# Hybrid encoder layer on one core: the MLP's split features move to the left stage pool of SBUF, its squared features to the right one

## The chip, the cores and the metric

The kernel runs on one core of a Trainium2 chip. The metric is the device time of one execution in microseconds (us). Beside it stands a profile of one execution, with its own time.

## The reference, cut to what matters

One encoder layer on 512 tokens of width 1024, all in float32: adaLN vectors, a mixer (a Hyena branch and a dilated attention branch, one output projection), a residual, and then the part that the change touches, the MLP:

```
h = rmsnorm(x, g_pre_mlp) * (1.0 + sc2) + sh2          # (512, 1024)
f = jnp.square(jax.nn.relu(h @ w_mlp1)) @ w_mlp2       # hidden width 4096
x = x + gt2 * rmsnorm(f, g_post_mlp)
```

## The kernel before, in words

**Precision.** Every matmul operand is split into a high and a low part of type fp32r (`whi`/`wlo` for weights, `h2h`/`h2l` for the normalised input of the MLP, the two halves of a tile `ha` for the hidden features). A product is three matmuls (`mm3`, line 610): high by high, high by low, low by high. ScalarE (ACT) makes the high part by a copy, VectorE (DVE) or GpSimd (POOL) the low part by a subtraction (`lo_of`, line 607).

**The MLP in blocks.** `hidden` (line 1392) computes one of 8 blocks of 512 hidden features: 8 x 4 x 3 matmuls of 128x128 by 128x512 into four PSUM banks `pm` (block 0 in two halves of 256 columns), then for each bank ACT applies the relu into a tile `hid` and DVE squares it in place. A `hid` tile holds two banks' worth, `[128, 2, 512]` float32, 4 KB of each partition.

The blocks are used in pairs. `products` (line 1492) takes one pair as a 2 x 2 block matrix and computes it with seven products in the manner of Strassen and Winograd, instead of eight. Each product reads two `ha` tiles (4 KB each), which `split_a` (line 1420) makes from `hid` or from a difference `dif` of `hid` tiles; it is 4 x 2 x 3 = 24 matmuls into two banks `pf`, with a slice of `ha` as the stationary operand and 512 columns of a weight tile as the moving one. Three pairs go that way; between the products lie the quarter blocks of the next pair (lines 1561 to 1567). The fourth pair (lines 1571 to 1598) is done directly: eight tiles `ha` in the list `parts` (one for every 128 hidden features), 2 x 8 x 4 x 3 = 192 matmuls, and after it the norm and the store of the output.

**Where tiles lie.** Two tile pools are shared out by stages. The left region, above the fixed pools, holds in turn `basis`, `wx` and, in the MLP, `hp`; the right region, at the upper end of SBUF, holds in turn `xp`, `hT`, `att` and, in the MLP, `mp` (lines 578 to 581). A pool opens when nothing of the pool before it is in use any more. In the program before, the byte addresses in each partition are: tag `cv` (among others `h2h`, `h2l`, and the filters' `fh`, the Hyena's `th`) 26,464 to 71,520; tags `vx` and `w` (weights `whi`, `wlo`) 92,000 to 135,008; tag `qk` (the tiles `nb`) 135,008 to 151,392; tag `H` (`mh`, `ml` in the output projection) 151,392 to 169,824; left region (`fb` in `basis`, output weights in `wx`, then `hp`) 171,872 to 196,512; right region (`hh`, `hl` in `hT`, `ma` in `att`, then `mp`) 196,576 to 229,344.

Before, `hp` holds 6 slots of `hid` and `mp` 8 slots of `ha`:

```
two = plan.tile("hp", "hid", 6, [P, 2, 512], F32, "hid")     # line 1408, in hidden
a = plan.tile("mp", "ha", 8, [P, 2, 2, 256], F32R, "ha")     # line 1423, in split_a
a = plan.tile("mp", "ha", 8, [P, 2, 512], F32R, "ha")        # line 1573, the last pair
```

**What sets the order.** Every operation is recorded and then put in order by a list scheduler (`Plan.order`, line 291): at each step it takes, over the engines, the operation that can start first by its own estimates of durations, with priorities by the longest path behind it and by a bonus that falls from one product or quarter block to the next (`begin`, line 1458). A new tile needs a free slot of its tag, and only the first tiles in recorded order, as many as there are free slots, may take one (`slot_time`, line 331). The engines then work in that order, each one in sequence.

Of the kernel before, what the change touches and what calls it, by code (L numbers as in the profile page):

```python
# [11 lines left out]
F32 = mybir.dt.float32  # L12
F32R = mybir.dt.float32r
# [12 lines left out]
P = 128  # L26
# [533 lines left out]
def tile_hymba_layer(ctx, tc, t, out):  # L560
    nc = tc.nc
    plan = Plan(nc)
# [23 lines left out]
    def S(tag, s="u", dt=F32):  # L586
        return plan.tile(HOME.get(tag, "up"), tag, NB[tag], [P, 512], dt, s)

    def R(tag, s="r"):
        return S(tag, s, F32R)  # L590
# [16 lines left out]
    def lo_of(eng, lo, full, hi):  # L607
        eng.tensor_tensor(out=lo, in0=full, in1=f(hi), op=ALU.subtract)

    def mm3(ps, lh, ll, rh, rl, start, stop):  # L610
        pe.matmul(ps, lh, rh, start=start, stop=False)
        pe.matmul(ps, lh, rl, start=False, stop=False)
        pe.matmul(ps, ll, rh, start=False, stop=stop)
# [8 lines left out]
    def wload(src):  # L622
        raw = S("raw", "raw")
        pre_loads.append(sp.dma_start(raw, src))
        hi, lo = wpair()
        act.copy(hi, raw)
        lo_of(vp, lo, raw, hi)
        return hi, lo
# [291 lines left out]
    for tt in range(4):  # L920
        for hf in range(2):
            a = S("x", "x")
# [18 lines left out]
    for d in range(8):  # L941
# [3 lines left out]
        a = S("vx", "xnT")  # L945
# [6 lines left out]
    for c in range(4):  # L952
# [4 lines left out]
        for d in range(2 * c, 2 * c + 2):  # L957
            hi = R("h", "hh")
            lo = R("h", "hl")
            a = xnT[d]  # L960
# [208 lines left out]
    for tt in range(4):  # L1169
        b3 = vb[tt].rearrange("p (h d) -> p h d", h=NH)  # L1170
        for g in range(2):
            a = R("cv", "vh")
# [84 lines left out]
    for hp2 in range(4):  # L1257
        (qh, ql), (kh, kl) = qk[hp2]
        a = S("vx", "att")
# [57 lines left out]
    for tt in range(4):  # L1317
        for hf in range(2):
            a = S("qk", "xr")
# [72 lines left out]
    def hidden(cc, banks, res):  # L1392

        for kk in range(0, 8, 2) if cc else (0,):
            if cc == 0:
                ws = [wload(w_1[k * P:(k + 1) * P, 0:512]) for k in range(8)]
            else:
                ws = {k: wload(w_1[k * P:(k + 1) * P, cc * 512:cc * 512 + 512]) for k in (kk, kk + 1)}
            for ts in HALF if cc == 0 else (slice(0, 512),):
                for k in range(8) if cc == 0 else (kk, kk + 1):  # L1400
                    for i in range(4):
                        s = slice(i * P, (i + 1) * P)
                        mm3(banks[i][:, ts], ws[k][0][:, s], ws[k][1][:, s], h2T[k][0][:, ts], h2T[k][1][:, ts], k == 0, k == 7)
            if kk < 6 and cc:
                yield
        for i in range(4):
            if i % 2 == 0:
                two = plan.tile("hp", "hid", 6, [P, 2, 512], F32, "hid")
                res.append(two)
            r = two[:, i % 2]  # L1410
            act.activation(r, banks[i], AF.Relu)
            vp.tensor_tensor(out=r, in0=r, in1=r, op=ALU.mult)
        yield
# [6 lines left out]

    def split_a(src):

        a = plan.tile("mp", "ha", 8, [P, 2, 2, 256], F32R, "ha")
        act.copy(a[:, 0], src)
        lo_of(vp, a[:, 1], src, a[:, 0])
        return a
# [28 lines left out]
    hid = {cc: [] for cc in range(2 * NS)}  # L1455
# [7 lines left out]
    def block(cc):  # L1463
        plan.group += 1
        gen = hidden(cc, PS4(cc == 0, "pm"), hid[cc])
        for _ in range(4 if cc else 1):
            begin()
            next(gen)
            yield
# [22 lines left out]
    def products(sb):  # L1492
# [45 lines left out]
        def first(k):  # L1538

            a = split_a(minus(0, A21, A22, k))  # L1540
            minus(2, A11, X[0], k)
            minus(1, A21, A11, k)
            return a

        same = lambda A: lambda k: split_a(A[k])
        product(3, same(A11), load("b", 0, 1))
        yield
# [6 lines left out]
        product(1, same(X[2]), more("s", 1, 1))  # L1554
        yield
        product(7, lambda k: split_a(minus(0, A12, X[2], k)), more("d", 1, 0))
        yield
        product(6, same(X[1]), more("s", 0, 1))
# [11 lines left out]

    parts = []
    for kk in range(8):
        a = plan.tile("mp", "ha", 8, [P, 2, 512], F32R, "ha")
        src = hid[2 * NS - 2 + kk // 4][kk % 4 // 2][:, kk % 2]
        act.copy(a[:, 0], src)
        lo_of(vp, a[:, 1], src, a[:, 0])
        parts.append(a)
    BLOCK = {(0, 0): 7, (0, 1): 5, (1, 0): 2, (1, 1): 6}
    for hf in range(2):
        plan.group += 1  # L1580
        banks = PS4(1 - hf, "pf")
        for ks, tts in (((0, 1, 2, 3), ((0, 1, 2, 3),)), ((4, 5, 6, 7), ((0,), (1,), (2,), (3,)))):
            begin()
            ws = [wload(w_2[(NS - 1) * 1024 + k * P:(NS - 1) * 1024 + (k + 1) * P, hf * 512:hf * 512 + 512]) for k in ks]
            for us in tts:
# [7 lines left out]
                a = acc[BLOCK[tt // 2, hf], tt % 2]  # L1593
# [48 lines left out]
```

## Time and profile before

| | before |
|---|---|
| time, median of 3 runs | 733.45 us (733.18 to 733.83) |
| the profiled execution's own time | 732.56 us |
| its span, first to last instruction | 730.8 us |
| PE (TensorE matmul) busy | 705.9 us, 97% of the span, 3576 instructions |
| DVE, ACT, POOL busy | 536.4, 357.9, 149.5 us |
| chain that ended last | PE 85%, DVE 6%, DMA 4%, ACT 3% |

Busy time is the union of an engine's instructions. Matmuls overlap in the records (each is shown from its start to the modelled end of its results), so the time that one costs is read from start to start, or from the length of a run divided by its matmuls, and not from the duration of one. PEld is the loading of stationary operands, which lies beside the matmuls. All operations recorded through the helper carry its line, L516, so tiles are told apart by name: `pm` is the first MLP matmul, `pf` the second one.

### The profile page before, as it was taken

The numbers are of one execution on the slowest core, as the hardware profiler recorded it, in microseconds if no ns is written. First come the engines' busy times: TensorE is split into PE (matmuls) and PEld (weight loads), VectorE is DVE, ScalarE is ACT, GpSimd is POOL, SyncE is SP. The second block draws the span as 40 slices with busy tenths as digits, with TensorE's granted clock in tenths as the row PEclk, the third lists the DMA queues.
The fourth block names the chain that finished last, engine by engine and source line by source line (L and its number), as shares of the span: only waits on it lengthen the run. The fifth ranks groups of instructions, "written<-read, shape, count | busy, mean of one in ns | idle before, by whom it ended". The sixth has DMA issues, their size and how long they took to land.

```text
span 730.8 us, 10377 instructions
## 1 busy us (share of the span) xinstructions
PE 705.9 (97%) x3576; PEld 570.2 (78%) x3576; DVE 536.4 (73%) x987; ACT 357.9 (49%) x691; POOL 149.5 (20%) x149
## 2 busy tenths in 40 slices
PE   5999999999999998999999999999999999999995
PEld 2667878988888876777888888888888888878884
DVE  5498883999799678999786875645667485686745
ACT  5536443225214258899675444645355254463421
POOL 0120500203031123333021023300252033321100
PEclk9999999999999999999999999999999999999998
DMA  9996325342623365253122667733785356833103
GB/s 292 360 392 208 105 93 199 93 163 88 188 87 117 114 197 165 87 173 101 59 73 87 202 158 178 154 87 126 170 167 130 116 141 157 163 102 124 49 30 115
DMA packets 60788, 106.13 MB, mean 145 GB/s; under 512 B 6429, under 2 KB 14877, under 8 KB 60480
## 3 DMA queue, kind: packets, MB, share of 16 engines
q1 hardware_dynamic: 52672, 88.44, 37.1%
q0 software_dynamic: 7920, 16.98, 12.0%
q8 instruction: 28, 0.46, 0.3%
q14 instruction: 24, 0.20, 0.1%
q10 hardware_dynamic: 144, 0.06, 0.0%
HBM read 101.00 MB, written 4.46 MB: 144 GB/s over the span
## 4 chain that ended last, share of the span: by engine, by line
PE 85%; DVE 6%; DMA 4%; ACT 3%; issue 1%; SPq 1%; POOL 0%; DVEq 0%; ACTq 0%; POOLq 0%
PE pm L516 23%; PE pf L516 22%; PE pj L516 17%; PE pw L516 6%; PE pH L516 4%; PE inv L516 2%; PE pav L516 2%; PE s L474 2%; DMA raw<-in_w_in_dram 2%; PE pe L516 2%; DMA raw<-in_w_ada_dram 2%; PE ptr L462 2%; PE po L516 1%; DMA x<-in_x_dram 1%; PE pa L516 1%
## 5 line engine op out<-in xcount | busy, mean ns | idle before, releaser
L516 PE MATMUL pf<-whi,ha 128*128 128x512 f32 x464 | 143.2, 395 | 0.0
L516 ACT CAST whi<-raw 128x512 fp32r<-128x512 f32 x144 | 87.8, 621 | 76.4 <-PE pj L516 28.2
L516 DVE TENSOR_TENSOR wlo<-raw,whi 128x512 fp32r<-128x512 f32 x124 | 85.8, 704 | 35.1 <-ACT whi L516 15.8
L516 PEld LDWEIGHTS pf<-whi,ha 128*128 128x128 f32 x464 | 87.4, 188 | 20.4 <-issue 0.2
L516 DVE TENSOR_TENSOR wlo<-braw,whi 128x512 fp32r<-128x512 f32 x79 | 57.1, 726 | 47.6 <-ACT whi L516 34.2
L516 PE MATMUL pm<-h2h,whi 128*128 128x512 f32 (+1 forms) x288 | 89.1, 368 | 0.7 <-DVE y L516 0.5
L516 PE MATMUL pm<-h2l,whi 128*128 128x512 f32 (+1 forms) x288 | 89.5, 368 | 0.3 <-POOL h2l L516 0.3
L516 PE MATMUL pm<-h2h,wlo 128*128 128x512 f32 (+1 forms) x288 | 88.7, 367 | 0.0
L516 PE MATMUL pf<-wlo,ha 128*128 128x512 f32 x232 | 82.4, 396 | 0.0
L516 ACT CAST whi<-braw 128x512 fp32r<-128x512 f32 x84 | 50.9, 621 | 62.5 <-DMA braw<-in_w_mlp_dram 29.7
L516 POOL DMA_DIRECT2D braw<-in_w_mlp_dram x48 | 41.9, 908 | 152.8 <-DVE wlo L516 131.4
L516 PEld LDWEIGHTS pm<-h2h,whi 128*128 128x128 f32 x288 | 53.1, 189 | 11.5 <-ACT h2h L516 1.4
L516 PEld LDWEIGHTS pm<-h2l,whi 128*128 128x128 f32 x288 | 53.2, 189 | 10.0 <-POOL h2l L516 0.7
L516 PEld LDWEIGHTS pm<-h2h,wlo 128*128 128x128 f32 x288 | 53.3, 189 | 9.0
L516 POOL TENSOR_TENSOR wlo<-raw,whi 128x512 fp32r<-128x512 f32 x20 | 27.0, 1352 | 136.8 <-ACT whi L516 61.2
L516 PEld LDWEIGHTS pf<-wlo,ha 128*128 128x128 f32 x232 | 43.7, 188 | 10.5 <-issue 0.2
L516 DVE SCALAR_TENSOR_TENSOR acc<-raw,vec,acc 128x512 f32<-128x512 f32 x56 | 43.9, 783 | 8.5 <-DMA raw<-in_w_ada_dram 8.2
L516 PE MATMUL pj<-hh,whi 128*128 128x512 f32 x96 | 35.2, 397 | 0.8 <-ACT hh L516 0.8
L516 PE MATMUL pj<-hl,whi 128*128 128x512 f32 x96 | 36.0, 400 | 0.0
L516 PE MATMUL pj<-whi,hh 128*128 128x512 f32 x96 | 35.1, 400 | 0.4 <-DVE y L516 0.4
L516 PE MATMUL pj<-hh,wlo 128*128 128x512 f32 x96 | 35.4, 397 | 0.0
L516 POOL TENSOR_TENSOR sc<-sc,st 128x512 f32<-128x512 f32 x21 | 23.7, 1146 | 55.2 <-DVE st L516 47.3
(276 smaller groups left out, 1457.7 us busy)
## 6 DMA issues: line engine op xcount, KB each, us to landing
raw<-in_w_ada_dram SPq DMA_DIRECT2D x96, 256.0 KB, 3.4
raw<-in_w_mlp_dram SPq DMA_DIRECT2D x80, 256.0 KB, 3.0
raw<-in_w_in_dram SPq DMA_DIRECT2D x48, 256.0 KB, 3.1
braw<-in_w_mlp_dram POOLq DMA_DIRECT2D x48, 256.0 KB, 4.7
braw<-in_w_mlp_dram SPq DMA_DIRECT2D x36, 256.0 KB, 3.0
raw<-in_w_out_dram SPq DMA_DIRECT2D x16, 256.0 KB, 2.6
H<-hd SPq DMA_DIRECT2D x9, 256.0 KB, 4.5
x<-in_x_dram SPq DMA_DIRECT2D x8, 256.0 KB, 5.4
```

Source lines behind the costliest of these rows:

```text
L462: plan.nc.tensor.transpose(out.ap()[:, i * P:(i + 1) * P], v.ap(), ident.ap())
L474: plan.nc.tensor.matmul(out.ap(), ts[i][0].ap(), ts[i][1].ap(), start=i == 0, stop=i == n - 1)
L516: getattr(e, meth)(*[real(a) for a in args], **{k: real(a) for k, a in kw.items()})
```

## The change

The tags swap pools. `hid`, which ACT writes and DVE, ACT and POOL read, goes to the right pool `mp` and has 8 slots in place of 6. `ha`, which PE reads as its stationary operand, goes to the left pool `hp` and has 6 slots in place of 8. The last pair needs eight `ha` tiles at once: six take `hp`, and the last two take slots of the tag `hid` in `mp`. All slots are 4 KB, so the pools keep their sizes.

```
-                two = plan.tile("hp", "hid", 6, [P, 2, 512], F32, "hid")
+                two = plan.tile("mp", "hid", 8, [P, 2, 512], F32, "hid")
...
-        a = plan.tile("mp", "ha", 8, [P, 2, 2, 256], F32R, "ha")
+        a = plan.tile("hp", "ha", 6, [P, 2, 2, 256], F32R, "ha")
...
     for kk in range(8):
-        a = plan.tile("mp", "ha", 8, [P, 2, 512], F32R, "ha")
+        a = plan.tile(*(("hp", "ha", 6) if kk < 6 else ("mp", "hid", 8)), [P, 2, 512], F32R, "ha")
```

No instruction is added or removed. The scheduler sees other numbers of slots.

## Rows read from the trace of the kernel before

**Rows 1.** The page, span in 40 slices: busy tenths, and PE's granted clock.
```profile
PE   5999999999999998999999999999999999999995
PEclk9999999999999999999999999999999999999998
```

**Rows 2.** Busy time by stretch of the MLP: us, engines, granted clock, DMA.
```profile
core 0: us, PE busy (x) PEld busy (x) DVE busy (x) ACT busy (x) POOL busy (x), PEclk, DMA share, GB/s
440.00:480.00 40.00, 40.00 (x175) 32.70 (x175) 22.81 (x36) 21.51 (x40) 10.77 (x13) 1.00 0.72 158
...
640.00:680.00 40.00, 40.00 (x175) 32.42 (x174) 30.51 (x45) 19.84 (x35) 8.99 (x7) 1.00 0.33 103
680.00:722.00 42.00, 42.00 (x182) 34.05 (x181) 22.19 (x38) 9.07 (x22) 2.60 (x2) 1.00 0.16 57
```

**Rows 3.** Chain of waits from 427 us on: start us, us, piece, matmuls.
```profile
278 pieces in order of time: start us, us, what
...
465.56 5.45 PE pm L516 x24
471.01 5.59 PE pf L516 x24
476.59 5.46 PE pm L516 x24
...
667.41 4.19 PE pf L516 x18
673.00 4.09 PE pm L516 x18
...
678.49 42.78 PE pf L516 x184
```

**Rows 4.** Same chain, first and last piece of a finely mixed stretch.
```profile
503.17 0.23 PE pf L516
...
509.94 0.23 PE pm L516
```

**Rows 5.** Chain of waits in the mixer: input projection, four unbroken runs.
```profile
71.31 5.80 PE pj L516 x25
85.66 5.34 PE pj L516 x23
...
183.84 21.48 PE pj L516 x92
...
228.92 21.04 PE pj L516 x90
```

**Rows 6.** PE in order of time, filters: stationary `nb`; start us, us, instruction.
```profile
65.82 0.86 PE L516 MATMUL pH<-fh,nb 128*128 128x512 f32 x3
66.51 0.63 PE L516 MATMUL pH<-fl,nb 128*128 128x512 f32 x2
66.98 0.62 PE L516 MATMUL pH<-fh,nb 128*128 128x512 f32 x2
67.44 0.40 PE L516 MATMUL pH<-fh,sm 128*128 128x512 f32 x1
67.67 0.40 PE L516 MATMUL pj<-hh,wlo 128*128 128x512 f32 x1
```

**Rows 7.** PE in order of time: stationary `nb` and `fb` in turn, ends of it.
```profile
110.68 0.39 PE L516 MATMUL pH<-fl,fb 128*128 128x512 f32 x1
...
112.99 0.40 PE L516 MATMUL pj<-hh,whi 128*128 128x512 f32 x1
```

**Rows 8.** PE in order of time, Hyena: stationary `fb` alone, ends of it.
```profile
125.46 0.40 PE L516 MATMUL po<-tl,fb 128*128 128x512 f32 x1
...
127.78 0.40 PE L516 MATMUL pj<-hh,wlo 128*128 128x512 f32 x1
```

**Rows 9.** PE in order of time, output projection: moving weights in `wx`.
```profile
297.61 0.63 PE L516 MATMUL pw<-whi,mh 128*128 128x512 f32 x2
298.08 0.62 PE L516 MATMUL pw<-wlo,mh 128*128 128x512 f32 x2
298.54 0.63 PE L516 MATMUL pw<-whi,ml 128*128 128x512 f32 x2
```

**Rows 10.** What reads and writes tile `ha`: durations ns min/median/max, first and last start.
```profile
L516 PE MATMUL pf<-whi,ha x464: 387/395/404, 427.8 to 722.0; 128*128 128x512 f32 x155
L516 PE MATMUL pf<-wlo,ha x232: 389/393/798, 428.3 to 721.8; 128*128 128x512 f32 x116
L516 ACT CAST ha<-hid x26: 612/618/642, 403.4 to 680.6; 128x512 fp32r<-128x512 f32 x26
L516 DVE TENSOR_TENSOR ha<-hid,ha x24: 678/685/1252, 406.1 to 681.2; 128x512 fp32r<-128x512 f32 x24
L516 ACT CAST ha<-dif x24: 615/621/625, 421.2 to 627.3; 128x512 fp32r<-128x512 f32 x24
...
  PE pf L516: 5.3, 5
```

**Rows 11.** ACT in order of time: the last pair's casts to `ha`.
```profile
676.25 0.61 ACT L516 CAST ha<-hid 128x512 fp32r<-128x512 f32 x1
...
679.02 1.13 ACT L516 CAST ha<-hid 128x512 fp32r<-128x512 f32 x2
...
680.57 0.62 ACT L516 CAST ha<-hid 128x512 fp32r<-128x512 f32 x1
```

## The prediction

> **What bounds the kernel now.** I read the span in slices first, then the MLP by stretches, then the chain of waits, then PE in order of time. In the slices PE is at nine tenths from the second one to the last but one, with the clock at its upper level, 2.4 GHz, throughout [rows 1]. In the MLP it is closer still: in every stretch from 440 to 722 us PE is busy for the whole of it at a granted clock of 1.00, while DVE is busy 53 to 76% and ACT 22 to 54% [rows 2]. The reader is to see that no wait is left here that a free slot could end. From 427 us the chain is a file of PE runs that follow one another, and what the MLP costs is the number of its matmuls times the step from one start to the next.
>
> That step is the one thing in which the two kinds of run differ. A quarter block `pm` of 24 matmuls takes 5.45 us, 227.1 ns each; a product `pf` of 24 takes 5.59 us, 232.9 ns each, and the last 184 take 42.78 us, 232.5 ns each [rows 3]. Form, clock and order (high, low, high) are the same. The operands lie elsewhere: `pm` reads weights and `h2h`/`h2l`, all below byte 135,008; `pf` reads the same weight slots and `ha` in the right region, above 196,576. In a stretch where `pm` and `pf` alternate one by one, 29 steps from 503.17 to 509.94 us, the mean is 233.4 ns, so that a `pm` beside a `pf` costs as much as a `pf` [rows 4]. The change moves `ha`, and so it can change this step.
>
> **Part by part.** *No instruction comes or goes*, on any engine or queue; no DMA moves. ACT and DVE write the same bytes to other addresses. I cost that at nothing; the cover is PE, which never waits for them, and with DVE at up to 76% of a stretch [rows 2] a few per cent on its instructions would still be hidden.
>
> *`ha` in the left region.* 464 and 232 matmuls read `ha` [rows 10], 696; of the last pair's 192 the quarter that reads the last two tiles, 48, stays in the right region, so 648 move to bytes 171,872 to 196,512. The trace before has no `pf` from there, but it has other fp32r matmuls of 512 columns with an operand at or near these bytes:
> - both operands low: 227.1 ns (`pm`) [rows 3].
> - moving low, stationary `nb` in tag `qk`, 135,008 upwards (and once a low `sm`): 8 steps in 1.85 us, 231.3 ns [rows 6].
> - moving low, stationary `nb` and `fb` (184,192 to 196,480) in turn: 10 steps in 2.31 us, 231.0 ns [rows 7].
> - moving low, stationary `fb` alone: 10 steps in 2.32 us, 232.0 ns [rows 8].
> - moving in `wx` (171,872 upwards), stationary `H` (151,392 to 169,824), so all of it in the left part but none low: 4 steps in 0.93 us, 232.5 ns [rows 9].
> - moving `hh`/`hl` in the right region, stationary low: 25 in 5.80 us and 23 in 5.34 us, 232.0 and 232.2 ns; moving low, stationary in the right region: 92 in 21.48 us and 90 in 21.04 us, 233.5 and 233.8 ns [rows 5].
>
> So the border of the quick step seems to lie near byte 135,000 and not between the left and the right region: every run with one operand above it steps in 231 to 234 ns, and `hp` lies wholly above it. The nearest rows to the new place are the three with a low moving operand and a stationary one in the left region's upper part, 231.3, 231.0 and 232.0 ns; I take their mean, 231.4. Against 232.5 that is 1.1 ns x 648 = 0.7 us less. The ends are 227.1 (as `pm`: 3.5 us less, and more with the neighbours, below) and 233.8 ns (0.8 us more).
>
> On the skill: the Trainium skill (SBUF — State Buffer, "SBUF: two separate sides") says that TensorE's ports never wait for anyone, and its page TensorE: Matmul & The Clock Gate ("Step-by-step: what each phase is for") gives the stationary and the moving operand a read port each. By these rules the place of `ha` would not matter. Rows 3 speak against them in so far as the same form takes 227.1 ns in one place and 232.9 ns in another; the rules have no term for that. What they would give is the third rival.
>
> *Six slots of `ha` in place of eight.* A product takes two, so products can be prepared three deep and not four. A product and the quarter block beside it make some 11 us (5.59 + 5.45) [rows 3], so a tile can be cast at the latest about two such rounds, 22 us, before PE wants it; making it takes a cast of 0.62 us and a subtraction of 0.69 us [rows 10], with hand-overs 2 to 3 us. ACT waits for a `pf` slot in front of its casts today 5 times, 5.3 us in all [rows 10], and PE does not notice; more such waits would hold up the weight casts behind them in ACT's queue by a few us, against the same 22 us. The tightest place is the last pair: its fifth and sixth tile are cast from 676.25 us [rows 11], and a slot for them has to come from the last product, whose run of 18 matmuls ends at 671.6 us (667.41 + 4.19) [rows 3]. Were that product later by a whole quarter block, 4.09 us, the casts would still start about when they do, and PE has the first four tiles to work on meanwhile, 4 x 4 x 3 = 48 matmuls, 11.2 us. The cost is nothing; with that cover gone, it would be one wait of 2 to 4 us.
>
> *Eight slots of `hid` in place of six.* This frees relu and square earlier. As PE waits for neither, it gives nothing. The last pair's two tiles in these slots need `hid` tiles of the third pair gone, which are read for the last time before the last cast of a `dif`, 627.3 us [rows 10].
>
> *The order.* With other slot counts the scheduler will order the MLP anew in places. A `pm` in an unbroken run costs 227.1 ns, one beside a `pf` 233.4, and the `pf` there some 0.8 ns more than in a run. The chain from 427 us has 278 pieces [rows 3], nearly all changes between `pm` and `pf`, so about 130 `pm` pay this. Fifty more or fewer such pairs are 7.1 ns x 50 = 0.4 us either way.
>
> **Sum.** The profiled execution took 732.56 us: 730.8 of span and 1.8 around it, which stays. Less 0.7 us that is 731.9. The median of the runs is 0.9 us above the profiled one, so 732.7 us by the clock of the median.
>
> **The rivals.**
> 1. *The left region reads as `pm` does.* What counts would be the region that the pool allocator calls right, or the exact start of it, and the 231 to 232.5 ns of rows 6 to 9 would come from small matmuls and waits around them in the mixer. For it: `pm` is the only long unbroken run there is with both operands on the left. Against it: rows 7 to 9 have four to ten steps in sequence with nothing else between and do not come down to 227, while runs of 24 `pm` that begin right behind a `pf` have it as their mean [rows 3]. It would give 648 x (232.5 - 227.1) = 3.5 us and 130 `pm` neighbours x 6.3 = 0.8 us: 732.56 - 4.3 + 0.9 = 729.1 us.
> 2. *Slower: a finer mix.* Fewer products ready ahead make the scheduler fill in `pm` one by one. There are 7 x 96 = 672 `pm` of 512 columns; about 130 sit in front of a `pf` now, 540 do not. Each that changes sides costs 7.1 ns with its partner, so 3.8 us at most; half of them give 1.9 us, and if the slot gain of 0.7 us fails too, 735.4 us, or 734.7 with it; I put it at 735.2 us. It decides from about 300 more pairs on (2.2 us of 7.1 ns each, with the 0.7 us gained). For it: the mixed stretch of rows 4 shows that the scheduler does this. Against it: the long runs of rows 3 are set by the bonus for each product and block, which the change does not touch.
> 3. *It does nothing.* `ha` in `hp` steps as before, 232.5 ns, and the order hardly moves: 733.4 us. This is also what the two rules of the Trainium skill named above would make of the change.
>
> **How the numbers follow.** My forecast, a step of 231 to 233.5 ns, has 0.56 (its own range 731.6 to 734.3 us, with 0.4 us of order either way); rival 1 has 0.20, rival 2 has 0.12, rival 3 has 0.12. About 0.2%, 1.5 us, is what a measurement of this kernel can tell from no change. Faster than 731.98 us: rival 1 and a tenth of my forecast's share with a lucky order, 0.27. Slower than 734.92 us: rival 2 and a little of the forecast, 0.14. Between, 0.59. The range has to hold rival 1, whose lower edge with 0.4 us of order is 728.7 us, and my forecast; above, it stops at 734.6 us and leaves out most of rival 2.
>
> **What would show it.** Right: unbroken runs of 24 `pf` take 5.54 to 5.60 us, and the last 180 or so step in 231 to 233 ns; PE is busy for the whole of the stretches from 440 to 720 us; `pm` runs stay at 5.45 us. Rival 1: `pf` runs of 24 in 5.45 us and mixed stretches at 227 ns. Rival 2: many more than 278 pieces in the chain from 427 us. The prediction is wrong in kind if PE waits for `ha` or for a weight anywhere between 440 and 720 us, or if the time comes out below 731 us with `pf` still above 231 ns.

## The result and the profile after

The changed kernel takes 729.28 us, median of 7 runs (728.72 to 731.98), beside 733.81 us of the kernel before on the same chip (7 runs, 732.54 to 736.17): a ratio of 0.9945, 95% interval 0.9932 to 0.9957. That is 4.5 us less, three times what a measurement can tell from no change. It lies inside my range of 728.7 to 734.6 us, but not at the forecast of 732.7: the first rival, 729.1 us, is what came.

The page of the kernel before, its rows of busy time (engine busy us, instructions; then a group of instructions with its count, busy us and mean ns of one):
```profile
PE 705.9 (97%) x3576; PEld 570.2 (78%) x3576; DVE 536.4 (73%) x987; ACT 357.9 (49%) x691; POOL 149.5 (20%) x149
...
L516 PE MATMUL pf<-whi,ha 128*128 128x512 f32 x464 | 143.2, 395 | 0.0
L516 PEld LDWEIGHTS pf<-whi,ha 128*128 128x128 f32 x464 | 87.4, 188 | 20.4 <-issue 0.2
```
The same rows of the page after:
```profile
PE 701.2 (96%) x3576; PEld 569.5 (78%) x3576; DVE 534.5 (73%) x989; ACT 357.2 (49%) x691; POOL 146.2 (20%) x147
...
L516 PE MATMUL pf<-whi,ha 128*128 128x512 f32 x464 | 136.0, 390 | 0.0
L516 PEld LDWEIGHTS pf<-whi,ha 128*128 128x128 f32 x464 | 87.2, 188 | 18.5 <-issue 0.2
```
As many matmuls as before, 4.7 us less busy time of PE, and the recorded matmul that reads `ha` is shorter, while the load of its stationary slice keeps its 188 ns. The chain of waits after, from 427 us on, which answers to [rows 3] (start us, us, piece, matmuls):
```profile
266 pieces in order of time: start us, us, what
...
465.91 5.44 PE pm L516 x24
471.35 5.44 PE pf L516 x24
476.79 5.44 PE pm L516 x24
...
664.11 4.53 PE pf L516 x20
669.55 4.53 PE pm L516 x20
674.99 42.80 PE pf L516 x187
```
A product of 24 matmuls now costs what a quarter block of 24 costs, 5.44 us or 226.7 ns a matmul. The last run alone is slower, 42.80 / 187 = 228.9 ns: a quarter of it reads the two tiles that stayed in the right region. The finely mixed stretch of [rows 4], PE in order of time after:
```profile
502.92 0.39 PE L516 MATMUL pf<-whi,ha 128*128 128x512 f32 x1
503.15 0.39 PE L516 MATMUL pm<-h2h,whi 128*128 128x512 f32 x1
...
509.95 0.39 PE L516 MATMUL pm<-h2h,whi 128*128 128x512 f32 x1
```
From 502.92 to 509.95 us there are 31 steps, 226.8 ns each, in place of 233.4: the `pm` beside a `pf` became quick with it. By stretches, the answer to [rows 2] (us, then busy time of PE, PEld, DVE, ACT, POOL with counts, granted clock, DMA):
```profile
440.00:480.00 40.00, 40.00 (x178) 33.15 (x177) 23.54 (x37) 22.02 (x40) 11.28 (x13) 1.00 0.75 163
640.00:680.00 40.00, 40.00 (x178) 33.15 (x177) 31.79 (x48) 19.80 (x35) 6.44 (x5) 1.00 0.33 105
680.00:722.00 42.00, 38.48 (x168) 31.27 (x167) 22.44 (x42) 9.93 (x25) 0.00 (x0) 1.00 0.16 57
```
PE still waits for nothing and the granted clock is still 1.00 (the upper level, 2.4 GHz); in 40 us it starts 178 matmuls and not 175. In the last stretch it is done 3.5 us before the end. So the gain is all in the step. The profiled span fell by 3.5 us only (730.8 to 727.3), in good part because this execution reached the same filter matmuls of [rows 6] 0.8 us later, at 66.65 in place of 65.82 us, before any instruction that the change touches.

### The profile page after: what moved, and what is told of

It is laid out like the page before. It is cut to its first block, busy times and chain, and to the rows that moved or that the text cites. A ratio compares the mean times of both kernels' runs of the same rounds, so it can differ in the third digit from the quotient of the medians.

```text
span 727.3 us, 10366 instructions
## 1 busy us (share of the span) xinstructions
PE 701.2 (96%) x3576; PEld 569.5 (78%) x3576; DVE 534.5 (73%) x989; ACT 357.2 (49%) x691; POOL 146.2 (20%) x147
## 4 chain that ended last, share of the span: by engine, by line
PE 84%; DVE 8%; DMA 3%; ACT 3%; issue 1%; SPq 0%; DVEq 0%; POOL 0%; ACTq 0%; POOLq 0%
PE pm L516 23%; PE pf L516 22%; PE pj L516 17%; PE pw L516 6%; PE pH L516 4%; PE inv L516 2%; PE pav L516 2%; PE s L474 2%; PE pe L516 2%; DMA raw<-in_w_ada_dram 2%; PE ptr L462 2%; PE po L516 1%; DMA raw<-in_w_in_dram 1%; DMA x<-in_x_dram 1%; DVE pr L516 1%
## 5 line engine op out<-in xcount | busy, mean ns | idle before, releaser
L516 PE MATMUL pf<-whi,ha 128*128 128x512 f32 x464 | 136.0, 390 | 0.0
L516 PE MATMUL pf<-wlo,ha 128*128 128x512 f32 x232 | 77.3, 391 | 0.0
L516 DVE TENSOR_TENSOR acc<-pf,acc 128x512 f32<-128x512 f32 x30 | 20.4, 689 | 20.1 <-PE pf L516 20.1
```

What stands on the lines that cost most here:

```text
L516: getattr(e, meth)(*[real(a) for a in args], **{k: real(a) for k, a in kw.items()})
```

## The experiments

My first theory after the result was that of the rival: either the right region as such is slow, or what counts is the byte at which an operand starts. The two hang together in both kernels, because the pools start at different remainders. I give a tile's start, as the program allots it, modulo 256: 171,872 = 671 x 256 + 96, and the weights, `h2h`/`h2l`, `nb`, `mh` and the left region all start at 96; 196,576 = 767 x 256 + 224, so the right region starts at 224; `fb` at 128. Slots are multiples of 256 bytes apart. "Apart" below is the distance between the start of the stationary and of the moving operand. Before, `pf` was 128 apart; after, 0, but for the last two tiles. Each experiment was run in 5 rounds; times are medians, ratios to the kernel before with 95% intervals.

### `ha` stays in the right region, and the fixed operand tiles move by 128 bytes

The kernel before, with 128 bytes laid ahead of the fixed operand tiles and one 32-byte slot fewer in a pool of small tiles behind them, so that the left region moves by 96 bytes. Weights, `h2h`/`h2l`, `nb`, `mh` and `fb` now start at 224 as the right region does; `wx` starts at 192.

```
-        return plan.tile("tiny", tag, 16, [P, 8], F32, s)
+        return plan.tile("tiny", tag, 16 if tag == "t1" else 15, [P, 8], F32, s)
...
+    pad = C("pad", [P, 32], F32)
+    pool.memset(pad, 0.0)
```

> The kernel before with 128 bytes of padding in the fixed pool, so that every tag of the fixed pools (weights, h2h, mh, nb) starts 128 bytes higher; one st slot fewer makes room. ha stays in the right region at bytes 196,576 to 229,344, but its start is now the same modulo 512 (480) as that of the weight tiles, as are hh, hl and ma. Theory A (the step is quick when stationary and moving operand start at the same byte modulo some power of two up to 512): runs of 24 pf take 5.44 us instead of 5.59, pj runs go from 232 to 234 ns a matmul to about 227, and the time falls by 4.4 us for the MLP and up to 3.5 us for the mixer: 726 to 729 us against 733.5. Theory B (the right region is slow to read): nothing changes, pf 5.59 us, 733.5 us. Theory C (number of slots): nothing changes, 733.5 us.

Measured: 727.09 us (725.78 to 728.41), ratio 0.9909 (0.9895 to 0.9922). The chain of waits of this kernel, in the MLP:
```profile
465.43 5.44 PE pm L516 x24
470.87 5.44 PE pf L516 x24
...
675.36 41.72 PE pf L516 x184
```
And in the mixer, beside [rows 5]:
```profile
72.33 5.67 PE pj L516 x25
86.44 5.21 PE pj L516 x23
...
184.25 20.87 PE pj L516 x92
...
228.73 20.66 PE pj L516 x90
```
With `ha` in the right region throughout, `pf` takes 226.7 ns, the last 184 too (41.72 / 184). The input projection, whose `hh`/`hl` lie in the right region, falls as well, the long runs from 233.5 and 233.8 to 226.8 and 229.6 ns. The right region is not slow. This kernel beats both, since it also speeds the mixer, which the change leaves alone (its four runs of [rows 5] are 5.80, 5.34, 21.48 and 21.04 us after as before).

### `ha` in the left region, 128 bytes further

The changed kernel, with 128 bytes at the head of the left pool, so that `ha` starts at 224 and the weights at 96. Nothing else moves against the changed kernel.

```
+    pool.memset(plan.tile("hp", "pad", 1, [P, 32], F32, "pad"), 0.0)
```

> The kernel after with 128 bytes of padding in front of ha in the left pool: ha at 172,000 to 196,576, still in the left region, but at 480 modulo 512 where the weights are at 352. Theory A: pf goes back to 232 to 233 ns a matmul (24 in 5.58 us), and the time to 733 us, as before the change. Theory B: pf stays at 226.7 ns, 729.3 us. Theory C: 729.3 us.

Measured: 733.72 us (732.78 to 734.8), ratio 1.0 (0.9991 to 1.0009). The chain of waits:
```profile
266 pieces in order of time: start us, us, what
...
466.28 5.45 PE pm L516 x24
471.73 5.59 PE pf L516 x24
...
679.00 43.47 PE pf L516 x187
```
The whole gain is gone with 128 bytes, in a chain of 266 pieces as in the changed kernel. The left region is not quick, and the new order and slots do not give the 4.5 us.

### `ha` in the left region, 64 bytes further

As above with `[P, 16]`: `ha` at 160, weights at 96.

> The changed kernel with 64 bytes laid ahead of the six ha tiles in the left region, so that they start at 416 modulo 512 where the weights start at 352: 64 bytes apart. Nothing else moves. If any difference that is not 0 modulo 256 costs the longer step, pf in the left region takes 231 to 235 ns a matmul as with 32 and 128 bytes, and the time is that of the kernel before, 733 to 735 us. If the rule is about a finer grain (starts equal modulo 64), the step is 226.7 ns and the time 728 to 730 us. If some differences of offset cost less than others, the step lies between, 228 to 230 ns, and the time near 731 us.

Measured: 733.82 us (732.83 to 735.6), ratio 0.9999 (0.999 to 1.0008). The chain of waits:
```profile
468.00 5.47 PE pm L516 x24
473.46 5.60 PE pf L516 x24
...
680.10 43.50 PE pf L516 x187
```
5.60 / 24 = 233.3 ns: 64 bytes apart is as dear as 128 in a run. Where `pm` and `pf` alternate one by one it is not; the ends of such a stretch, PE in order of time:
```profile
505.47 0.40 PE L516 MATMUL pf<-whi,ha 128*128 128x512 f32 x1
...
511.91 0.40 PE L516 MATMUL pf<-whi,ha 128*128 128x512 f32 x1
```
That is 28 steps in 6.44 us, 230.0 ns, half way between the two prices, where the mixed stretch of [rows 4] at 128 apart has 233.4.

### The changed kernel with the 128 bytes ahead of the fixed tiles

The edit of the first experiment on the changed kernel. The weights start at 224, six `ha` tiles in the left region at 192 (32 apart), the last two in the right region at 224 (0 apart).

> The kernel after with the same padding as the first run: the weights at 480 modulo 512, ha in the left pool at 448 (32 bytes off), hh, hl, ma and the two last ha tiles in the right region at 480. Theory A with a grain of 32 bytes or finer: pf slows to 231 to 233 ns, while pj in the mixer gains 3 us: 730 us. Theory A with a coarser grain: pf stays at 227, pj gains: 726 us. Theory B: pf stays at 226.7 ns, pj as before: 729.3 us.

Measured: 731.95 us (730.71 to 734.81), ratio 0.9976 (0.9966 to 0.9986). The chain of waits in the MLP:
```profile
464.51 5.45 PE pm L516 x24
469.96 5.59 PE pf L516 x24
...
677.23 43.43 PE pf L516 x187
```
32 apart is dear too, 232.9 ns. Within the last run both prices stand side by side: steps between matmuls on left tiles average 233.3 ns (124 steps), those between matmuls on the two tiles in the right region 226.7 ns (29 steps). In the changed kernel it is the other way round: 226.7 ns left (118 steps), 232.7 ns right (29). What this kernel wins against the one before comes from the input projection: its 400 steps from one `pj` to the next average 227.7 ns in place of 232.5, 1.9 us in all, for instance 20.70 us for 90 `pj` at 228.69 us in place of 21.04. I had expected 3 us of it.

### Slots alone

The kernel before with six slots of `ha` in the right pool; the last pair takes its seventh and eighth tile from the slots of `hid` in the left pool.

```
-        a = plan.tile("mp", "ha", 8, [P, 2, 512], F32R, "ha")
+        a = plan.tile(*(("mp", "ha", 6) if kk < 6 else ("hp", "hid", 6)), [P, 2, 512], F32R, "ha")
```

> The slots alone: 6 of ha in place of 8, both tags in their pools of before, only the last two ha tiles in hid slots of the left pool. Theory C (slots or order brought the gain): 729.3 us. Theories A and B: 733.4 us, less some 0.3 us for the 48 matmuls whose ha now lies in the left pool.

Measured: 734.86 us (733.83 to 736.19), ratio 1.0009 (1.0 to 1.0018). `pf` runs of 24 take 5.59 us, in a chain of 266 pieces as after. Fewer slots of `ha` and the order that follows cost nothing that could hide a gain or make one. The profiled execution, 735.43 us, has a granted clock of 0.98 from 262 to 345 us, ahead of the MLP, and the quickest three runs, 733.83 to 733.88 us, lie at the median of the kernel before, 733.76, so the 0.0009 need not come from the slots. The 29 steps between the two left tiles, 0 apart, averaged 231.6 ns here, in short bursts among matmuls that are 128 apart: equal starts were not enough in such a burst.

### Weights and right region 256 apart

The kernel before with four small fixed tiles (32 bytes each) moved into the pool of small tiles. The weights start at 224 modulo 256, but 256 bytes from the right region's start when counted modulo 512; `fb` and `wx` keep their places, 160 from the weights and 128 from `mh`.

```
-    a1 = C("a1", [P, 8], F32)
+    a1 = C("a1", [P, 8], F32, "tiny")
...
-    sc2, sh2, a2 = C("sc2", [P, 8]), C("sh2", [P, 8]), C("a2", [P, 8])
+    sc2, sh2, a2 = [C(n, [P, 8], F32, "tiny") for n in ("sc2", "sh2", "a2")]
```

> The kernel before with four small vectors moved from the first fixed pool to the last one, so that the weights, h2h, mh and nb start 128 bytes lower: 224 modulo 512, and the right region with ha, hh, hl, ma, at 480, is 256 bytes off. Theory A with a period of 256 bytes: pf and pj step in 227 ns, 727 us as with the shift by 128 upwards. Theory A with a period of 512 bytes or more: pf stays at 231 to 234 ns and the time at 733.5 us. Theory B (right region slow) is also 733.5 us, but it has fallen with the shift upwards.

Measured: 728.16 us (726.5 to 729.02), ratio 0.9917 (0.9904 to 0.9931). The chain of waits in the MLP:
```profile
463.79 5.44 PE pm L516 x24
469.23 5.44 PE pf L516 x24
...
673.52 41.72 PE pf L516 x184
```
PE in order of time, the filters' run that answers to [rows 6] and the Hyena's that answers to [rows 8]:
```profile
66.30 0.84 PE L516 MATMUL pH<-fh,nb 128*128 128x512 f32 x3
66.98 0.62 PE L516 MATMUL pH<-fl,nb 128*128 128x512 f32 x2
67.44 0.62 PE L516 MATMUL pH<-fh,nb 128*128 128x512 f32 x2
67.89 0.40 PE L516 MATMUL pH<-fh,sm 128*128 128x512 f32 x1
...
125.62 0.40 PE L516 MATMUL po<-tl,fb 128*128 128x512 f32 x1
...
127.95 0.39 PE L516 MATMUL pj<-hh,wlo 128*128 128x512 f32 x1
```
256 apart is as good as 0. The Hyena's ten steps on `fb`, 160 apart, stay at 2.33 us, 233 ns; in the first experiment, where `fb` starts as the weights do, the same ten took 2.27 us (125.93 to 128.20 us). The seven `nb` steps are 0 apart here as before: 227.1 ns (66.30 to 67.89), where they took 231.4 before (65.82 to 67.44 in [rows 6]). Their operands kept their distance; of their neighbours the `pj` went from 128 to 256 apart.

### All starts equal, in both kernels

The first experiment with 32 bytes at the head of `wx`, and the changed kernel with the same and 32 bytes at the head of `hp`. Every large fp32r operand of PE but the inverse transform's `ib` starts at 224.

```
+    pool.memset(plan.tile("wx", "padx", 1, [P, 8], F32, "pad"), 0.0, urgent=SOON)
...
+    pool.memset(plan.tile("hp", "pad", 1, [P, 8], F32, "pad"), 0.0, urgent=SOON)
```

> The kernel before, shifted by 128 bytes as in the first experiment, and 32 bytes of padding in front of the output weights in wx, so that these too start at 480 modulo 512; ha in the right region. Theory A: the output projection's unbroken pw runs (ma stationary, half the weights in wx) go from 232 to 227 ns a matmul; at most 96 + 96 matmuls of 5 ns, some of them hidden between small ones: 0.3 to 0.9 us less than the shift alone, 726.5 us.

> The kernel after, with the same shift and the same padding in front of wx and of ha: everything that PE reads in fp32r, but the inverse transform's ib, starts at 480 modulo 512. Theory A: with the starts equal the place of ha is worth nothing, so the same time as the kernel before with the same padding, 726.5 us within 0.7 us. If the right region were slower in some way of its own, this one is quicker by 1 us or more.

Run beside them, the changed kernel again:

> The kernel after on the same chip and in the same rounds as the padded ones: 729.3 us, 0.55% below the kernel before, and 2 to 3 us above the kernels with all starts equal (theory A), since pj, pH and po in the mixer still start 128 or 32 bytes apart.

Measured: 727.88 us (727.29 to 732.2), ratio 0.9926 (0.9907 to 0.9945), for the kernel before with equal starts; 728.3 us (726.98 to 733.85), ratio 0.9938 (0.992 to 0.9956), for the changed one with equal starts; 729.2 us (728.77 to 730.34), ratio 0.9937 (0.9924 to 0.995), for the changed one as it is. Once the starts are equal, the pools may be swapped or not: the intervals of the first two lie over each other. The chain of waits of the changed kernel with equal starts shows both regions at one price:
```profile
470.82 5.44 PE pf L516 x24
...
674.88 42.40 PE pf L516 x187
```
42.40 / 187 = 226.7 ns, six tiles left and two right. That padding is worth 2 to 3 us over the change was not borne out here: its medians are 0.9 to 1.3 us lower and the intervals overlap. Nor did the 0.3 to 0.9 us that I expected of the padding in `wx` over the first experiment show, 727.88 us beside 727.09. These kernels scatter upwards, and the profiled execution of the first of them took 732.2 us, with a granted clock of 0.98 over a stretch of the mixer (columns as above):
```profile
180.00:262.00 82.00, 79.27 (x411) 66.79 (x410) 65.29 (x121) 23.86 (x40) 15.78 (x15) 0.98 0.39 121
```
Before and after have 1.00 there. In the same execution the granted clock is 0.98 again from 262 to 345 us, and so it is there in the profiled executions of the first experiment, of the 64 bytes and of the slots alone, the last of which has no padding. From 427 to 717 us, in the MLP, all have 1.00. Why the clock drops in some executions was not tried.

The output projection fits in part only. In the kernel before, the run of [rows 9] has both operands at 96 and yet took 232.5 ns. With all starts equal (the first of the three, PE in order of time):
```profile
300.78 0.62 PE L516 MATMUL pw<-whi,mh 128*128 128x512 f32 x2
301.24 0.62 PE L516 MATMUL pw<-wlo,mh 128*128 128x512 f32 x2
301.71 0.63 PE L516 MATMUL pw<-whi,ml 128*128 128x512 f32 x2
302.18 0.60 PE L462 MATMUL ptr<-ident,sc 128*128 128x128 f32 x4
```
Six steps in 1.40 us, 233 ns. It is a run of six between small matmuls. Over the whole trace the 105 steps from one `pw` to the next average 229.2 ns here and 232.0 before, so part of them became quick. The head of a longer run behind small matmuls shows the same, here in the first experiment, with both operands at 224:
```profile
255.93 0.39 PE L516 MATMUL pj<-whi,hh 128*128 128x512 f32 x1
...
257.32 0.39 PE L516 MATMUL pj<-wlo,hh 128*128 128x512 f32 x1
...
257.77 0.39 PE L516 MATMUL pj<-whi,hh 128*128 128x512 f32 x1
...
262.08 0.39 PE L516 MATMUL pj<-wlo,hh 128*128 128x512 f32 x1
```
Its first 6 steps average 231.7 ns, the 19 from 257.77 us on 226.8. The 229.6 ns of the 90 `pj` above is of this kind too: from 233.35 us on that run steps in 226.8 ns. Together with the bursts in the slots experiment this bounds the rule: long runs with equal starts became quick, short ones among other matmuls did not always, perhaps because some end within such a head. The short bursts on the two right tiles in the changed kernel with the 128 bytes ahead were quick, 226.7 ns. What makes a head slow was not tried.

## Why the prediction was right in its range and wrong in its forecast

- *No instruction comes or goes, PE bounds the MLP by count times step.* Right: 3576 matmuls both times, PE busy for the whole of the stretches from 440 to 680 us.
- *The step on `ha` in the left region, 231.4 ns.* This is the step that failed. It measured 226.7 ns: 648 x (232.5 - 226.7) = 3.8 us in place of 0.7, and the some 130 `pm` beside a `pf` gave another 130 x (233.4 - 226.8) = 0.9 us. Together some 4.6 us, against 4.5 measured and 4.7 in PE's busy time. The two products stood in the working as rival 1; I gave it 0.20. My forecast's own range, 731.6 to 734.3 us, does not hold 729.28: the stated range does so only because it was drawn wide enough for that rival.
- *The border near byte 135,000.* False. I sorted the rows by place, because place was what the change named. Sorted by the distance of the two starts, most of them fall in line: `pj` 128 apart, `fb` 32 apart, all slow; `pm` 0 apart, quick. The runs of [rows 6], but for the one on `sm`, and [rows 9] were 0 apart and slow all the same. They are runs of eight and six; the first became quick when only its neighbours changed, and the second, slow even with all starts equal, is no longer than the slow head shown above. A mean over such runs was too weak a witness for 648 matmuls in long runs, for which the one fitting row was `pm`.
- *The rival's reasons.* It named the right region or its exact start. The place as such is out (the first two experiments); the start holds, as a distance between two operands. That `pm` was the only long run with both operands in the left part was true, but not the reason. That small matmuls made rows 6 to 9 slow may hold for rows 6 and 9; `fb` in rows 7 and 8 was 32 apart.
- *Slots and order, nothing to 0.4 us.* Right. The chain has 266 pieces where it had 278 [rows 3], the slots alone measured a ratio of 1.0009, and casts to `ha` wait for `pf` 5 times, 5.1 us in all, as before [rows 10]. The second rival, a finer mix, did not come.
- *The last two tiles.* I counted them as no gain, which is right: 232.7 ns against 226.7.
- *The rules of the Trainium skill.* The Trainium skill (TensorE: Matmul & The Clock Gate, "Step-by-step: what each phase is for") has the load of the next stationary operand take nothing from the running matmul's reads, since each has a read port. The place of `ha` did indeed not matter by itself. But moving it by 128 bytes cost 5.59 - 5.44 = 0.15 us for every 24 matmuls, which that rule has no term for; the measurement decides.

What goes on inside stays open. Shown is that the step of a run depends on the distance of the two starts, that 0 and 256 bytes apart are quick, and that 32, 64, 128 and, in one run of ten, 160 are not. Whether the reads of the stationary slice and of the moving columns meet in the memory is a guess that no run here tested: the recorded load keeps its 188 ns either way.

## What to carry to other kernels

When the same form of matmul takes two different steps in one trace, write down the start of both operands modulo 256 before reasoning about where they lie. In a kernel bound by PE, aligning all pools to one remainder is worth trying: here a pad of 128 bytes ahead of the fixed operand tiles gave a ratio of 0.9909, more than swapping two pools. And a change that moves buffers for one reason can win by another: pad it back by a few bytes and see whether the gain stays.

## What the runs showed of the hardware that was not expected

The step of an unbroken fp32r run, 128x128 by 128x512 at a granted clock of 1.00, is 226.7 ns with the operands' starts 0 or 256 bytes apart, and 232.9, 233.3, 232.9 ns at 32, 64 and 128 apart: some 6 ns, 2.7%. A matmul with equal starts beside one that is 128 apart pays as well: 233.4 ns mean in the mixed stretch before [rows 4], 226.8 after. Beside one that is 64 apart the mean is 230.0, so there it seems not to pay. And a run with equal starts that follows small matmuls can take some steps, 231.7 ns each in the one shown, before it is quick.
